# Attention's loads and broadcasts moved behind other steps of the combining sequence

## The chip, the cores and the metric

One core of a Trainium2 chip (trn2) runs the whole program. The metric is device time in microseconds (us) of one execution, the median of several runs. Lower is better.

## The reference

One decoder layer on x of shape (1, 2048, 1024) in float32. A projection gives q, k, v, two gates and the inputs of a state-space branch. The part that matters here is attention: 16 heads of 64, three dilations (1, 4, 16), each a causal band of 129 steps, and the three results weighted by a softmax over their log-sum-exps:

```python
o1, l1 = dilated_window_attention(q, k, v, slopes, DILATIONS[0])
o2, l2 = dilated_window_attention(q, k, v, slopes, DILATIONS[1])
o3, l3 = dilated_window_attention(q, k, v, slopes, DILATIONS[2])
wts = jax.nn.softmax(jnp.stack([l1, l2, l3], axis=0), axis=0)
y_att = (wts[0][..., None] * o1 + wts[1][..., None] * o2 + wts[2][..., None] * o3)
y_att = rms_norm(y_att.reshape(Bsz, S, D_ATT) * jax.nn.silu(z_att), att_norm_g[layer])
```

The state-space branch, an output projection of both branches and a layer norm follow.

## The kernel before, in words

The program has three stages. The projections with the state-space branch take the first 1163 us or so. Attention follows to about 1653 us. The output projection with its norms ends the program.

**Attention** works on the heads in 8 pairs (`pr` 0 to 7). For each pair it goes through the three dilations `d` in turn (the code's d = 0 is dilation 16, d = 1 is 4, d = 2 is 1), each in 4 quarters `qd` of 2 halves: 24 half steps for a pair. A half step is recorded in three parts at different times: `scores` (TensorE products of q and k, VectorE bias and running minimum at L955, ScalarE exponentials at L961), two half steps later `transposes` (TensorE, copied by VectorE at L978 and L987), and three half steps later `values` (TensorE products with v at L1002, and after the second half two ScalarE copies of 128x256 from PSUM into `num`, at L1026, L1029 or L1032 by dilation). TensorE runs these in the order of recording, so the scores of the next pair's first half step stand three half steps ahead of its values.

**The operands of a pair.** `load_x` brings q and k (1 MB each, two sets of buffers that alternate between pairs), `load_v` brings `v` and, for d = 1 and 2, a shifted copy `vs` (about 1 MB each, three buffers of each name). All are DMAs that GpSimd (POOL) issues (L872, L888, L890). POOL also makes permuted copies of q (`permute`, L914 and L918).

**Combining.** When a pair is through, `statistics` writes its row statistics to DRAM, `gather` reads them back (L1060, a POOL DMA), and while the next pair runs `weights` turns them into softmax weights (VectorE, one exponential on ScalarE) and writes them to DRAM (`d_wd`, L1078, a DMA issued by SyncE, SP). These are then read back as broadcasts: `wb`, 128x2048, 1 MB for each dilation, each as two DMAs of 64 partitions (L1091, SP). POOL combines in six steps k = 0 to 5 (`combine`): steps 0, 1 and 3 multiply one dilation's `num` by its `wb` (L1093), steps 2 and 4 add (L1097), step 5 multiplies by the gate (L1108), and the result goes to DRAM. For the last pair VectorE does this instead, at the beginning of the output projection.

**What sets the order.** TensorE, VectorE, ScalarE and POOL execute in the order in which the Python code records. The table `STEPS` says at which half step (d, qd, half of `values`) which combining step of the pair before is recorded and which load behind it. POOL takes its rows one after the other: a combining step that waits for its broadcast holds every load recorded behind it. SP's DMAs are in an order that a scheduler sets.

In the loop, `weights` (two parts) is recorded at (0, 2, 1) and (0, 3, 0). `STEPS` has, for pair `pr`: v and vs of its own d = 2 at (0, 0, 0) and (0, 0, 1); at (1, 0, 0) step 0 and the next pair's q; at (1, 1, 0) step 1 and the next pair's k; at (1, 2, 0) step 2 and the next pair's v for d = 0; at (1, 3, 0) step 3; at (2, 0, 0) the next pair's v for d = 1; at (2, 1, 0) step 4 and its vs; at (2, 2, 0) step 5. For pair 7 the v and vs of d = 2 stand at (1, 0, 0) and (1, 0, 1).

The output projection (`product`, L1185 to L1187) multiplies split activations (`split`, L1149 to L1153) by the output weights. Its first products need no attention result; the later ones need pair 7's combined values.

## Time and profile before

| | |
|---|---|
| median of 3 runs | 2035.58 us (2030.0 to 2038.48) |
| the profiled execution | 2040.01 us, span 2037.9 us from the first to the last instruction |
| mean granted TensorE clock | 0.985 |
| share of the span: PE, DVE, ACT, POOL | 96%, 62%, 55%, 50% |
| DMA, whole program | 447.72 MB, mean 220 GB/s |

PE is TensorE, PEld its weight loads, DVE is VectorE, ACT is ScalarE, POOL is GpSimd; SPq and the like are the sequencers that issue DMAs. In a timeline row stand the start in us from the beginning of the span, the duration, engine, line, operation, the tiles written and read, how many instructions are merged into the row, and in brackets the idle time before it with what ended it. A wait put down to "issue" is one for which the profile shows no cause. PE's busy time counts pipelined products whose ends are modelled, so 96% is not a full array.

### The profile page before, as it was taken

How to read it: one execution, taken by the hardware profiler on the slowest of the kernel's cores; microseconds unless marked ns; L12 is line 12 of the kernel's file. 1: busy time of each engine (PE TensorE's matmuls, PEld its weight loads, DVE VectorE, ACT ScalarE, POOL GpSimd, SP SyncE). 2: the span in 40 equal slices, each digit the busy share in tenths (PEclk: the TensorE clock that was granted, in tenths of full speed). 3: DMA queues.
4: the chain of work that ended last, by engine and by line, in shares of the span. 5: the costliest groups of instructions: out<-in, count | busy, mean ns of one | idle time of the engine just before them, and what ended most of it. 6: DMA issues, size and time to landing. Idle time of an engine off the chain costs nothing.

```text
span 2037.9 us, 42696 instructions
## 1 busy us (share of the span) xinstructions
PE 1961.9 (96%) x16024; PEld 1598.2 (78%) x16024; DVE 1271.4 (62%) x3193; ACT 1128.9 (55%) x3066; POOL 1010.1 (50%) x866
## 2 busy tenths in 40 slices
PE   8999999999999999999999999998989989999998
PEld 7888879888888888988888776666766668888886
DVE  7555365777766665644454387787777756665553
ACT  4455333556556774456557488887878742222220
POOL 0366513666646767155555424667766652432222
PEclk9999999999999999999999999999999989999999
DMA  6688665565787776887888756777787799332210
GB/s 265 211 281 298 221 252 215 172 197 173 244 287 276 268 256 241 306 275 249 282 269 272 250 191 198 211 215 227 222 235 223 196 309 298 122 97 103 85 67 31
DMA packets 230286, 447.72 MB, mean 220 GB/s; under 512 B 40192, under 2 KB 112384, under 8 KB 218688
## 3 DMA queue, kind: packets, MB, share of 16 engines
q1 hardware_dynamic: 138352, 190.64, 29.5%
q0 software_dynamic: 43776, 160.49, 23.3%
q10 hardware_dynamic: 47952, 93.87, 15.0%
q8 instruction: 126, 2.06, 0.4%
q14 instruction: 80, 0.66, 0.1%
HBM read 301.91 MB, written 151.39 MB: 222 GB/s over the span
## 4 chain that ended last, share of the span: by engine, by line
PE 83%; DMA 5%; DVE 5%; ACT 4%; issue 2%; SPq 1%; POOL 0%; ACTq 0%; POOLq 0%; DVEq 0%
PE pp L260 13%; PE pp L264 13%; PE pp L262 13%; PE N L1002 6%; PE S L949 4%; PE S L1185 4%; PE S L1187 4%; PE S L1186 4%; PE pp L309 4%; PE T L976 3%; ACT P L961 2%; PE T L1185 2%; PE T L1186 2%; PE T L1187 2%; PE ss L309 2%
## 5 line engine op out<-in xcount | busy, mean ns | idle before, releaser
L217 POOL TENSOR_TENSOR w<-wr,w 128x512 fp32r<-128x512 f32 x217 | 285.4, 1326 | 277.0 <-ACT w L216 182.7
L961 ACT ACTIVATE P<-P,st 128x192 f32<-128x192 f32 (+1 forms) x768 | 323.9, 424 | 71.1 <-DVE st L955 67.2
L252 ACT COPY ev<-pp 128x512 f32<-128x512 f32 x200 | 117.2, 588 | 312.5 <-PE pp L264 275.3
L955 DVE CUSTOM_DVE_ANT_0 P<-S,tb 128x192 f32<-128x192 f32 (+1 forms) x768 | 206.8, 325 | 104.5 <-PE S L949 79.9
L272 DVE TENSOR_TENSOR ev<-pp,ev 128x512 f32<-128x512 f32 x152 | 101.2, 686 | 141.4 <-PE pp L264 91.8
L1093 POOL TENSOR_TENSOR wb<-num,wb 128x2048 f32<-128x2048 f32 x21 | 95.5, 4549 | 116.2 <-ACT P L961 63.1
L216 ACT CAST w<-wr 128x512 fp32r<-128x512 f32 x224 | 134.2, 621 | 28.6 <-DVE wr L211 13.3
L961 ACT ACTIVATION_READ_ACCUMULATOR P<-P,st 128x1 f32 x768 | 145.4, 189 | 0.0
L1002 PE MATMUL N<-PT,v 128*64 128x64 f32 (+1 forms) x1536 | 127.0, 262 | 13.7 <-ACT num L1026 10.4
L978 DVE COPY PT<-T 128x512 f32<-128x512 f32 x192 | 131.8, 687 | 4.0 <-PE T L976 3.9
L976 PE MATMUL T<-ident,P 128*128 128x128 f32 x768 | 129.7, 293 | 0.2 <-DVE PT L978 0.2
L976 PEld LDWEIGHTS T<-ident,P 128*128 128x128 f32 x768 | 83.1, 144 | 48.2 <-issue 23.9
L949 PE MATMUL S<-k,ex 64*64 64x192 f32 (+1 forms) x2048 | 113.8, 331 | 6.8 <-issue 6.8
L1002 PEld LDWEIGHTS N<-PT,v 128*64 128x64 f32 x1536 | 79.4, 139 | 51.8 <-ACT num L1026 20.2
L211 DVE TENSOR_TENSOR wr<-wr 128x512 f32<-128x512 f32 x128 | 113.0, 883 | 9.3 <-DMA wr<-w 5.4
L468 DVE SCALAR_TENSOR_TENSOR ss<-U,cw,ss 128x512 f32<-128x512 f32 x144 | 106.0, 751 | 2.9 <-ACT ss L464 0.6
L1161 DVE TENSOR_REDUCE tb<-P 128x128 f32<-128x1024 f32 x30 | 60.1, 2004 | 45.4 <-ACT P L1158 23.0
L1223 POOL TENSOR_TENSOR k<-k,wb 128x1024 f32<-128x1024 f32 x8 | 25.8, 3229 | 122.7 <-DVE k L1222 122.7
L949 PEld LDWEIGHTS S<-k,ex 64*64 64x64 f32 x2048 | 68.6, 138 | 19.5 <-issue 13.3
L594 ACT ACTIVATE mt<-csb,cs 128x128 f32<-128x128 f32 x256 | 79.0, 395 | 0.9 <-PE ss L634 0.8
L603 DVE TENSOR_TENSOR mt<-mt,ss 128x1024 f32<-128x1024 f32 x32 | 39.0, 1220 | 53.3 <-ACT mt L599 52.8
L260 PE MATMUL pp<-TB11h,w 128*128 128x512 f32 x176 | 69.6, 395 | 0.0
(484 smaller groups left out, 6013.0 us busy)
## 6 DMA issues: line engine op xcount, KB each, us to landing
wr<-w ACTq DMA_DIRECT2D x164, 256.0 KB
d_wc<-w SPq DMA_DIRECT2D x48, 512.0 KB
w<-d_wc POOLq DMA_DIRECT2D x48, 512.0 KB, 5.8
wb<-d_wd SPq DMA_DIRECT2D x48, 512.0 KB
d_wo<-wot POOLq DMA_DIRECT2D x32, 512.0 KB, 4.4
csb<-d_cs ACTq DMA_DIRECT2D x32, 512.0 KB
v<-d_v POOLq DMA_DIRECT2D x16, 1024.0 KB, 7.0
vs<-d_v POOLq DMA_DIRECT2D x16, 960.0 KB, 9.0
```

What stands on the lines that cost most here:

```text
L216: nc.scalar.copy(h, r)
L217: low.tensor_tensor(l, r, h.bitcast(F32), op=OP.subtract)
L260: nc.tensor.matmul(ps, w[:, 0, k], th[:, k], start=start and k == 0, stop=False, skip_group_check=not start)
L262: nc.tensor.matmul(ps, w[:, 0, k], tl[:, k], start=False, stop=False, skip_group_check=not start)
L264: nc.tensor.matmul(ps, w[:, 1, k], th[:, k], start=False, stop=(k == 3), skip_group_check=not start)
L309: nc.tensor.matmul(o, (th, tl)[j == 1][:, k, t], w[:, int(j == 2), k], start=start and r % 2 == k == j == 0, stop=(k == 3 and j == 2), ski ...
L949: nc.tensor.matmul(o, A["q"][d][64 * h:64 * h + 64, blk, 64 * a:64 * a + 64], kv, start=True, stop=True)
L955: nc.vector.tensor_tensor_reduce(P[:, h, cs], sp[h][:, cs], t, -0.125, 3.0e38, OP.add, OP.min, accum_out=stat(A, 0, d, h, blk))
L961: nc.scalar.activation(p, p, AF.Exp, bias=stat(A, 0, d, h, blk), scale=-1.0, accum_out=stat(A, 1, d, h, blk))
L976: nc.tensor.transpose(tp[:, h, i], P[:, h, 256 * i:256 * i + 128], ident)
L978: nc.vector.tensor_copy(pt, tp)
L1002: nc.tensor.matmul(o, l, r, start=start, stop=True, skip_group_check=True)
```

## The change

It has five parts.

1. `STEPS` is rewritten. For pair `pr`, v and vs of its own d = 1 are loaded at (0, 0, 0) and (0, 0, 1), behind the gather; v of its own d = 2 behind step 0 at (1, 0, 0), vs of d = 2 behind step 1 at (1, 1, 0); the next pair's q behind step 3 at (1, 3, 0), its k behind step 4 at (2, 0, 0), its v of d = 0 behind step 5, which is now at (2, 1, 0). Pair 7 follows the same table.
2. A broadcast is one DMA of 128 partitions. Step 0's is issued by SP after the last part of the weights. Steps 0 and 1 are cut in halves of 8 rows of 16, and between the halves POOL issues the next broadcast: step 1's inside step 0, step 3's inside step 1.
3. `weights` has three parts, at (0, 2, 1), (0, 3, 0) and (0, 3, 1), so its DRAM write comes one half step later. A subtraction, two multiplications and two additions move from VectorE to POOL; two minima and the reciprocal stay. Pair 7 keeps VectorE.
4. For d = 0 the second of the two copies into `num` goes from ScalarE to VectorE.
5. In the output projection the last pair's weights are recorded behind the first product and the third split, where they stood ahead of the first product; of the output weights' loads into buffers of that time, two entries of `LOADS` move from (2, 1, 0) and (2, 1, 1) to (2, 2, 0) and (2, 2, 1).

```diff
@@ -1023,7 +1023,8 @@
                 for i in range(2):
                     nm = A["N"][i][:, 0:256]
                     if d == 0:
-                        nc.scalar.copy(f2(num[:, 4 * qd + 2 * i:4 * qd + 2 * i + 2, :]), nm)
+                        copy = nc.vector.tensor_copy if i else nc.scalar.copy
+                        copy(f2(num[:, 4 * qd + 2 * i:4 * qd + 2 * i + 2, :]), nm)
                     elif d == 1:
                         o = num.rearrange("p (b s) (n a j) -> p n b a s j", b=4, a=2, j=16)[:, qd, 2 * i:2 * i + 2]
                         nc.scalar.copy(o, nm.rearrange("p (b a s j) -> p b a s j", b=2, a=2, s=4))
@@ -1062,20 +1063,29 @@
         def weights(A, part):
 
             m_, s_ = A["cm"][:, :, 0], A["cm"][:, :, 1]
+            eng = nc.vector if A["pr"] == 7 else nc.gpsimd
             if part == 0:
                 mm = A["mm"] = cm_.tile([128, 32], F32, name="mm")
                 nc.vector.tensor_tensor(mm, m_[:, 0], m_[:, 1], op=OP.min)
                 nc.vector.tensor_tensor(mm, mm, m_[:, 2], op=OP.min)
-                nc.vector.tensor_tensor(m_, mm[:, None, :].to_broadcast([128, 3, 32]), m_, op=OP.subtract)
+                eng.tensor_tensor(m_, mm[:, None, :].to_broadcast([128, 3, 32]), m_, op=OP.subtract)
+            mm = A["mm"]
+            if part == 1:
                 nc.scalar.activation(m_, m_, AF.Exp)
-                return
-            mm = A["mm"]
-            nc.vector.tensor_tensor(s_, s_, m_, op=OP.mult)
-            nc.vector.tensor_tensor(mm, s_[:, 0], s_[:, 1], op=OP.add)
-            nc.vector.tensor_tensor(mm, mm, s_[:, 2], op=OP.add)
-            nc.vector.reciprocal(mm, mm)
-            nc.vector.tensor_tensor(m_, m_, mm[:, None, :].to_broadcast([128, 3, 32]), op=OP.mult)
-            nc.sync.dma_start(dap(d_wd[A["pr"]], 0, [[32, 128], [2 * S, 3], [1, 32]]), m_)
+                eng.tensor_tensor(s_, s_, m_, op=OP.mult)
+                eng.tensor_tensor(mm, s_[:, 0], s_[:, 1], op=OP.add)
+                eng.tensor_tensor(mm, mm, s_[:, 2], op=OP.add)
+            if part == 2:
+                nc.vector.reciprocal(mm, mm)
+                eng.tensor_tensor(m_, m_, mm[:, None, :].to_broadcast([128, 3, 32]), op=OP.mult)
+                nc.sync.dma_start(dap(d_wd[A["pr"]], 0, [[32, 128], [2 * S, 3], [1, 32]]), m_)
+
+        def broadcast(A, k):
+
+            d = k - k // 2
+            wb = A["w", k] = cm_.tile([128, NR, NJ], F32, name="wb", bufs=3)
+            (nc.sync if A["pr"] == 7 or k == 0 else nc.gpsimd).dma_start(
+                f2(wb), dap(d_wd[A["pr"]], d * 2 * S, [[S, 2], [0, 64], [1, S]]))
 
         def combine(A, k):
 
@@ -1086,11 +1096,16 @@
             pu = lambda a: a.rearrange("p (n r j) -> p r n j", r=NR, j=8)
             if k in (0, 1, 3):
                 d = k - k // 2
-                wb = A["wb"] = cm_.tile([128, NR, NJ], F32, name="wb", bufs=3)
-                for h in range(2):
-                    nc.sync.dma_start(f2(wb[64 * h:64 * h + 64]),
-                                      dap(d_wd[pr], (d * 2 + h) * S, [[0, 64], [1, S]]))
-                eng.tensor_tensor(wb, A["num"][d], wb, op=OP.mult)
+                if last:
+                    broadcast(A, k)
+                wb, num = A.pop(("w", k)), A["num"][d]
+                A["wb"] = wb
+                if last or k == 3:
+                    eng.tensor_tensor(wb, num, wb, op=OP.mult)
+                else:
+                    eng.tensor_tensor(wb[:, 0:8], num[:, 0:8], wb[:, 0:8], op=OP.mult)
+                    broadcast(A, 2 * k + 1)
+                    eng.tensor_tensor(wb[:, 8:16], num[:, 8:16], wb[:, 8:16], op=OP.mult)
                 if k == 0:
                     A["acc"] = wb
             elif k < 5:
@@ -1226,13 +1241,13 @@
 
         O = {}
         pairs = {}
-        STEPS = {(0, 0, 0): (None, "v", 0, 2), (0, 0, 1): (None, "vs", 0, 2), (1, 0, 0): (0, "q", 1),
-                 (1, 1, 0): (1, "k", 1), (1, 2, 0): (2, "v", 1, 0), (1, 3, 0): (3, None, 0), (2, 0, 0): (None, "v", 1, 1),
-                 (2, 1, 0): (4, "vs", 1, 1), (2, 2, 0): (5, None, 0)}
+        STEPS = {(0, 0, 0): (None, "v", 0, 1), (0, 0, 1): (None, "vs", 0, 1), (1, 0, 0): (0, "v", 0, 2),
+                 (1, 1, 0): (1, "vs", 0, 2), (1, 2, 0): (2, None, 0), (1, 3, 0): (3, "q", 1), (2, 0, 0): (4, "k", 1),
+                 (2, 1, 0): (5, "v", 1, 0)}
         LOADS = {(0, 0, 0): ((8, None, "k_0"),), (1, 0, 1): ((9, None, "q_0"),), (1, 1, 0): ((10, None, "ex"),),
                  (1, 2, 0): ((11, None, "vs"),), (1, 2, 1): ((12, 0, "q_1"),), (1, 3, 0): ((13, 0, "v"),),
-                 (2, 0, 0): ((14, 0, "v"), (15, 0, "vs")), (2, 1, 0): ((12, 1, None), (13, 1, None)),
-                 (2, 1, 1): ((14, 1, None), (15, 1, None))}
+                 (2, 0, 0): ((14, 0, "v"), (15, 0, "vs")), (2, 2, 0): ((12, 1, None), (13, 1, None)),
+                 (2, 2, 1): ((14, 1, None), (15, 1, None))}
         todo = [(pr, d, qd, half) for pr in range(8) for d in range(3) for qd in range(4) for half in range(2)]
         pts = {}
         TA = 2
@@ -1270,8 +1285,10 @@
                         statistics(pairs[pr], 1)
                         gather(pairs[pr])
                     at = d, qd, half
-                    if pr and at in ((0, 2, 1), (0, 3, 0)):
-                        weights(pairs[pr - 1], qd - 2)
+                    if pr and at in ((0, 2, 1), (0, 3, 0), (0, 3, 1)):
+                        weights(pairs[pr - 1], 2 * qd + half - 5)
+                    if pr and at == (0, 3, 1):
+                        broadcast(pairs[pr - 1], 0)
                     if at == (0, 0, 0) and pr < 7:
                         pairs[pr + 1] = load_pair(pr + 1)
                     if pr and at == (0, 3, 0):
@@ -1284,8 +1301,6 @@
                         split(0, 1, parts=(1,))
                     if at in STEPS:
                         k, x, nx, *dd = STEPS[at]
-                        if pr == 7 and k is None and d == 0:
-                            x = None
                         if pr and k is not None:
                             combine(pairs[pr - 1], k)
                         if x and pr + nx < 8 and (pr or nx):
@@ -1293,8 +1308,6 @@
                                 load_v(pairs[pr + nx], x, dd[0])
                             else:
                                 load_x(pairs[pr + nx], x)
-                    if pr == 7 and at in ((1, 0, 0), (1, 0, 1)):
-                        load_v(pairs[7], ("v", "vs")[half], 2)
                     if at == (2, 2, 0) and pr < 7:
                         permute(pairs[pr + 1], 1)
                     if pr < 7:
@@ -1320,8 +1333,6 @@
             squares(0, 1)
             split(1, 1)
             squares(1, 1)
-            weights(A, 0)
-            weights(A, 1)
             ops = [(n, 1) for n in range(4)] + [(n, 0) for n in range(4)]
             ops += [(n, br) for n in range(4, 16) for br in (1, 0)]
             items = [(4 * j + k, hf) for j in range(2) for k, hf in
@@ -1353,6 +1364,9 @@
                 if i in splits:
                     j = splits[i]
                     split(*ops[j])
+                    if i == 0:
+                        for n in range(3):
+                            weights(A, n)
                     squares(*ops[j])
                     for m in (j + 2,) if 4 < j < 30 else ():
                         fetch_raw(*ops[m])
```

## The prediction

> **What bounds it.** I read the page first, then TensorE's waits, then, for attention, the timelines of PE, POOL and SP beside each other.
>
> ```profile
> span 2037.9 us, 42696 instructions
> ```
>
> ```profile
> PE N L1002 <- issue: 14.2, 6, 3.2
> PE N L1002 <- ACT num L1026: 10.4, 8, 1.7
> PE S L1185 <- ACT ex L1151: 8.2, 1, 8.2
> PE S L949 <- issue: 6.8, 5, 3.4
> ```
>
> The execution took 2040.0 us, 2.1 us outside its span and 4.4 us over the median of 2035.6; I sum against 2040.0 and carry the difference over. TensorE, the engine that ends last, waits little: 21.0 us for causes the profile does not name, 10.4 us for copies at the end of d = 0, and 8.2 us once at the beginning of the output projection. So attention runs at TensorE's pace, and a load that comes in time is free. The question is whether loads still come in time. Here are the points at which TensorE needs them. The first rows are the first score products of pairs 1, 5 and 7 (they read q and k); the row at 1424.54 opens the values of d = 1 in pair 4, those with 128x128 x4 open the values of d = 2 in pairs 4 and 6, and the one with vs right behind is the first to need vs.
>
> ```profile
> 1219.17 0.62 PE L949 MATMUL S<-k,q 64*64 64x128 f32 x16
> ...
> 1424.54 0.71 PE L1002 MATMUL N<-PT,v 128*64 128x128 f32 x8 [1.57 <-ACT num L1026]
> ...
> 1445.82 0.27 PE L1002 MATMUL N<-PC,v 64*64 64x64 f32 x2 [3.22 <-issue]
> ...
> 1448.76 0.69 PE L1002 MATMUL N<-PT,v 128*64 128x128 f32 x4
> 1449.24 0.42 PE L1002 MATMUL N<-PT,vs 128*64 128x64 f32 x4
> ...
> 1460.34 0.62 PE L949 MATMUL S<-k,q 64*64 64x128 f32 x16
> ...
> 1573.27 0.44 PE L1002 MATMUL N<-PT,v 128*64 128x128 f32 x4
> ...
> 1584.04 0.62 PE L949 MATMUL S<-k,q 64*64 64x128 f32 x16
> ```
>
> Six pairs take 1584.04 - 1219.17 = 364.9 us, 60.8 each. Now POOL and SP, which feed them: the first combining steps of pairs 1, 4 and 7 are those at 1252.01, 1434.45 and 1617.49.
>
> ```profile
> 1252.01 4.55 POOL L1093 TENSOR_TENSOR wb<-num,wb 128x2048 f32<-128x2048 f32 x1 [17.89 <-DMA wb<-d_wd]
> ...
> 1416.56 1.16 POOL L890 DMA_DIRECT2D v<-d_v  x1
> 1417.70 1.21 POOL L890 DMA_DIRECT2D vs<-d_v  x1
> 1434.45 4.55 POOL L1093 TENSOR_TENSOR wb<-num,wb 128x2048 f32<-128x2048 f32 x1 [15.54 <-ACT P L961]
> 1438.94 0.60 POOL L872 DMA_DIRECT2D q<-d_q  x1
> 1440.51 4.52 POOL L1093 TENSOR_TENSOR wb<-num,wb 128x2048 f32<-128x2048 f32 x1 [0.97 <-ACT P L961]
> 1444.98 0.61 POOL L872 DMA_DIRECT2D k<-d_k  x1
> 1445.61 4.55 POOL L1097 TENSOR_TENSOR wb<-wb 128x2048 f32<-128x2048 f32 x1
> ...
> 1617.49 4.56 POOL L1093 TENSOR_TENSOR wb<-num,wb 128x2048 f32<-128x2048 f32 x1 [15.39 <-ACT P L961]
> ```
>
> ```profile
> 1241.06 0.38 SPq L1078 DMA_DIRECT2D d_wd<-cm  x1
> 1243.54 5.18 SPq L1091 DMA_DIRECT2D wb<-d_wd  x6
> ...
> 1422.07 0.38 SPq L1078 DMA_DIRECT2D d_wd<-cm  x1
> 1427.24 3.67 SPq L1091 DMA_DIRECT2D wb<-d_wd  x6
> ...
> 1673.92 2.39 SPq L1091 DMA_DIRECT2D wb<-d_wd  x4
> ```
>
> POOL idles 15.5 us for the first broadcast and starts combining at 1434.45, call it C; the exponentials named as releaser were long done. From the issue at 1427.24 to C is 7.2 us, one landing. TensorE needs vs of d = 2 at 1449.24 = C + 14.8 and the next k at 1460.34 = C + 25.9. Before, d = 2's values were issued 17 us ahead of C and k 10.5 us after it: both early.
>
> **The change, part by part.** First what stands on POOL from the first combining step on, before (d_v_84 holds d = 0 and 2, d_v_85 holds d = 1; q_62 and k_70 are the next pair's):
>
> ```order
> L890 DMA vs<-d_v_84 128x15x128
> L1093 TENSOR_TENSOR wb<-num,wb 128x2048
> L872 DMA q<-d_q_62 128x2048
> L1093 TENSOR_TENSOR wb<-num,wb 128x2048
> L872 DMA k<-d_k_70 128x2048
> L1097 TENSOR_TENSOR wb<-wb 128x2048
> L888 DMA v<-d_v_84 32x16x128 x4
> L1093 TENSOR_TENSOR wb<-num,wb 128x2048
> ```
>
> And after, at the same place, from the broadcast (L1087) that now stands between the halves of step 0 (L1106, L1108):
>
> ```order
> L1087 DMA wb<-d_wd_120 128x1x2048
> L1108 TENSOR_TENSOR wb<-num,wb 128x1024
> L890 DMA v<-d_v_84 128x16x128
> L1106 TENSOR_TENSOR wb<-num,wb 128x1024
> L1087 DMA wb<-d_wd_120 128x1x2048
> L1108 TENSOR_TENSOR wb<-num,wb 128x1024
> L890 DMA vs<-d_v_84 128x15x128
> L1112 TENSOR_TENSOR wb<-wb 128x2048
> L1104 TENSOR_TENSOR wb<-num,wb 128x2048
> L872 DMA q<-d_q_62 128x2048
> L1112 TENSOR_TENSOR wb<-wb 128x2048
> L872 DMA k<-d_k_70 128x2048
> ```
>
> The d = 2 loads went from ahead of step 0 to behind steps 0 and 1, and k from behind two steps to behind five. Durations of the loads, from the page (last number: median us to landing) and, for q and k, from their own line (least, median, most), and the loads of pair 7, whose d = 2 values already stand behind its step 0, in the chain of waits:
>
> ```profile
> v<-d_v POOLq DMA_DIRECT2D x16, 1024.0 KB, 7.0
> vs<-d_v POOLq DMA_DIRECT2D x16, 960.0 KB, 9.0
> ...
> q<-d_q POOLq DMA_DIRECT2D x8, 1024.0 KB, 9.8
> k<-d_k POOLq DMA_DIRECT2D x8, 1024.0 KB, 6.6
> ```
>
> ```profile
> DMA to landing us min/median/max: 6.0/8.5/12.0
> ```
>
> ```profile
> 1623.21 13.54 DMA vs<-d_v
> ```
>
> *The chain from C.* Half of step 0 is 2.27 (4.55 / 2), so the second broadcast is issued at C + 2.3 and, at 7.2 to landing, lets step 1 start at C + 9.5; POOL is through with its half, two issues (0.6 and 1.2) and waits 3.2. Step 1 with an issue inside is 5.15: vs of d = 2 is issued at C + 14.6 and lands 9.0 later at C + 23.6, against C + 14.8: **8.8 us late**. The issue (1.2), step 2 and step 3 (4.55 each) lead to C + 25.0, q's issue to 25.6, step 4 to 30.1; k, issued there, lands 6.6 later at C + 36.7, against C + 25.9: **10.8 us late**. The third broadcast, issued at C + 11.8, is there by C + 19 and costs nothing. The two delays overlap: from the d = 2 values to the next scores TensorE takes 1584.04 - 1573.27 = 10.8 us, or 11.6 behind the stall at 1445.82 (1448.76 to 1460.34). From vs's landing that gives C + 23.6 + 11.1 = C + 34.7, 2.0 us ahead of k. So k is last, and I take 10.8.
>
> The clock is a reason for 11.6: behind that 3.22 us stall the window (column PEclk) reads half.
>
> ```profile
> 1448.00:1450.00 2.00, 2.00 (x22) 1.55 (x24) 1.63 (x8) 1.77 (x8) 2.00 (x1) 0.50 0.78 315
> ```
>
> The Trainium skill, TensorE: Matmul & The Clock Gate (Part 1), says that about 3.4 us of idling halves the clock until some 3.4 us of work. This rule speaks against the change, whose stalls are longer; the trace agrees with 0.50 behind 3.22 us.
>
> *C itself.* On SP the six broadcast DMAs become one, before and after:
>
> ```order
> L1078 DMA d_wd_120<-cm 128x3x32
> L1091 DMA wb<-d_wd_120 64x2048 x6
> ```
>
> ```order
> L1081 DMA d_wd_120<-cm 128x3x32
> L1087 DMA wb<-d_wd_120 128x1x2048
> ```
>
> The first broadcast was first in its queue before, so 7.2 stays. The weights' write comes half a step later, 1.9 us (half of the 3.75 between the copies below). It took 5.2 us to land in pair 4 (1422.07 to 1427.24) beside v and vs, 2.5 in pair 1. Since a pair's last loads are now issued well ahead of its end, the stretch around the gather should hold less traffic, and I take pair 1's 2.5: C moves by 1.9 - 2.7 = -0.8, with +1.9 as the other end. Each of six pairs costs 10.8 - 0.8 = 10.0: **60 us**.
>
> *Pair 7.* vs landed 13.5 after its issue, at C + 19.3 (1636.75 - 1617.49). After, it is issued at C + 15.2 (an output weight's load stands ahead, 0.6) and lands 9.0 to 13.5 later, C + 26.5 in the middle: 7.2 - 0.8 = **6.4 us**.
>
> *d = 0.* Copies sit 3.75 us apart:
>
> ```profile
> 1410.97 0.62 ACT L1026 COPY num<-N 128x256 f32<-128x256 f32 x2
> 1414.72 0.61 ACT L1026 COPY num<-N 128x256 f32<-128x256 f32 x2
> ```
>
> ScalarE loses one of two (0.31) a quarter, VectorE gains one. By bounds 0.3 less or 0.3 more a quarter, 1.2 a pair; any gain ends in the wait for k, so **0**. POOL's five small weight operations lie in its 15.5 us of idling: nothing. The loads of d = 1 take the place of those at 1416.56 and 1417.70: at the medians v lands at 1423.6, ahead of its first use at 1424.54, and vs at 1426.7, before the second quarter; a microsecond late would be swallowed by the wait for vs of d = 2.
>
> *The end.* Weights behind the third split remove the 8.2 us wait for ScalarE (and slow clock behind it, some 3 us). But the products that need pair 7's result still wait for its combining.
>
> ```profile
> 1685.11 4.49 DVE L1093 TENSOR_TENSOR wb<-num,wb 128x2048 f32<-128x2048 f32 x2
> ```
>
> It can start at 1673.92 + 7.2 = 1681.1 at the earliest, 4.0 sooner: **-4 us**, between 0 and -11.4.
>
> Sum: 60 + 6.4 - 4 = +62, 2102 for the profiled execution, 2098 on the median. The good ends: 6.0 to each landing takes 3.0 off a pair (1.2, 1.2 and 0.6), pair 7 costs 1.7, the end -11.4: 42 + 1.7 - 11.4 = +32, 2068. The bad ends: 8.5 each is 4.5 more a pair, C 2.7 more, pair 7 13.9, the end 0: 6 x 17.2 + 13.9 = +117, 2153; all at once is unlikely.
>
> **Rivals.** *Faster.* POOL keeps ahead of TensorE, and bursts of six broadcast DMAs, inside which the stall at 1445.82 lies, no longer hold TensorE: 21.0 + 8.2 less, 2006. It decides once C comes 10.0 us sooner still, at 1423.7. Against it: the weights' write was only issued at 1422.07, and it and a broadcast have to land first. 0.06.
>
> *Single transfers land soon.* A transfer alone may be quicker. With x for the two broadcasts and k, a pair costs 3x - 11: 7.0 at 6.0, 1.0 at 4.0, nothing at about 3.5, where POOL's own steps bound it. That gives 2032 (the end's 4 us alone) to 2068, the middle 2050. Against it: the second broadcast, behind the first, let step 1 start 6.1 us after C, and no q or k took less than 6.0. 0.11. The Trainium skill, DMA: Bandwidth & Descriptors (Anatomy of one DMA), gives 2.0 us plus bytes over 436 GB/s, 4.4 us for such a megabyte: 2.2 a pair, 4 us less for pair 7 and 4 at the end, an estimate of 2041 by that page; no row here is that quick.
>
> *Shared queue.* vs, issued while the third broadcast runs, takes 13.5 as in pair 7: C + 14.6 + 13.5 + 11.1 = C + 39.2 becomes last, 12.5 a pair, pair 7 8.6: 75 + 8.6 - 4 = +80, 2115. 0.14.
>
> **The numbers.** The forecast has 0.69, at 2098; alone it reaches from 2068 to 2120. The range of 2052 to 2120 adds the shared queue and the slower half of soon-landing transfers. A difference of 0.5%, 10 us, is about what can be told here. Faster by more: the first rival, 0.06. Within: the lower half of the second, 0.05. Slower: 0.89.
>
> **What would show it.** In the profile after: scores of one pair to the next near 70.8 us; two waits of TensorE in each pair, for vs at d = 2's first values and for k at the next scores; POOL waiting about 3 us between steps 0 and 1; C some 35 us behind a pair's first scores, as before; no 8.2 us wait for ScalarE. I am wrong if C comes 10 us sooner, or if vs and k land before TensorE asks.

## The result, and the profile after

The changed kernel takes 2536.64 us (median of 4 runs, 2533.29 to 2541.59); the kernel before, run beside it, 2032.94 us. The ratio is 1.2476, with a 95% interval of 1.2438 to 1.2513. The forecast was 2098, the range 2052 to 2120: slower was right, the size was not, by a factor of eight in the difference. The profiled execution has a span of 2531.5 us (2037.9 before) and a mean granted clock of 0.889 (0.985 before).

First TensorE's waits after (engine, tile and line, what was waited for; then us in total, times, the longest):

```profile
PE N L1002 <- DMA v<-d_v: 259.2, 11, 38.7
PE N L1002 <- DMA vs<-d_v: 213.6, 7, 33.1
PE S L1202 <- DVE num L1168: 36.9, 1, 36.9
PE S L1200 <- ACT num L1166: 17.2, 1, 17.2
```

These four sum to 526.9 us, more than the 493.6 us by which the span grew; the waits for causes not named (21.0 before) and for the copies of d = 0 (10.4) have gone. Two long waits in each pair, where the forecast had one for vs and one for k. They are 36 and 30 us long, and they are for v of d = 2, which was to be in time, and for vs; for k TensorE waits 0.2 us in the whole program. The first scores of pairs 1 and 7, and the two waits of pair 1:

```profile
1217.51 0.62 PE L949 MATMUL S<-k,q 64*64 64x128 f32 x16
...
1297.12 0.70 PE L1002 MATMUL N<-PT,v 128*64 128x128 f32 x4 [36.47 <-DMA v<-d_v]
...
1328.09 0.48 PE L1002 MATMUL N<-PT,vs 128*64 128x64 f32 x4 [30.27 <-DMA vs<-d_v]
...
1959.08 0.62 PE L949 MATMUL S<-k,q 64*64 64x128 f32 x16
```

A pair takes (1959.08 - 1217.51) / 6 = 123.6 us, 62.8 more than the 60.8 before; the forecast had 70.8. The reason stands on SP and POOL in the same pair:

```profile
1243.46 0.58 SPq L1087 DMA_DIRECT2D wb<-d_wd  x1
```

```profile
1267.49 2.34 POOL L1106 TENSOR_TENSOR wb<-num,wb 128x1024 f32<-128x1024 f32 x1 [26.38 <-DMA wb<-d_wd]
1269.77 0.87 POOL L1087 DMA_DIRECT2D wb<-d_wd  x1
1270.67 2.35 POOL L1108 TENSOR_TENSOR wb<-num,wb 128x1024 f32<-128x1024 f32 x1
1272.95 1.22 POOL L890 DMA_DIRECT2D v<-d_v  x1
1294.52 2.33 POOL L1106 TENSOR_TENSOR wb<-num,wb 128x1024 f32<-128x1024 f32 x1 [20.34 <-DMA wb<-d_wd]
...
1325.63 4.50 POOL L1104 TENSOR_TENSOR wb<-num,wb 128x2048 f32<-128x2048 f32 x1 [19.85 <-DMA wb<-d_wd]
```

A broadcast takes 24 us to land, from 1243.46 to 1267.49, and the second one 24.8 us; the forecast had 7.2. So C comes 17 us later than a landing of 7.2 would have it, step 1 starts 27.0 us behind C in place of 9.5, and POOL waits three times in each pair. v is issued at 1272.95 behind the second broadcast, and TensorE gets it at 1297.1, just after that broadcast has landed; most of it moves soon (279 GB/s in 1276 to 1278, 49 again in 1280 to 1282), and its rest lands only with the end of the broadcast. The line of the broadcasts that POOL issues has this for all 14, and the page this for v and vs (7.0 and 9.0 before):

```profile
DMA to landing us min/median/max: 24.6/27.5/31.6
```

```profile
v<-d_v POOLq DMA_DIRECT2D x16, 1024.0 KB, 11.7
vs<-d_v POOLq DMA_DIRECT2D x16, 960.0 KB, 13.0
```

Why one megabyte takes so long is in the windows (the window, its length, busy time of PE, PEld, DVE, ACT and POOL, the granted clock, the share of the 16 DMA engines, GB/s). After, while only a broadcast runs, and later with the rest of v:

```profile
1246.00:1248.00 2.00, 2.00 (x48) 1.53 (x46) 1.67 (x9) 1.49 (x9) 0.00 (x0) 1.00 0.12 41
...
1290.00:1292.00 2.00, 0.00 (x0) 0.00 (x0) 0.00 (x0) 0.00 (x0) 0.00 (x0) 0.50 0.13 53
```

and before, in the burst of six DMAs:

```profile
1428.00:1440.00 12.00, 11.71 (x253) 8.93 (x249) 10.07 (x51) 10.40 (x46) 5.09 (x2) 1.00 1.00 218
```

The share is 0.12 to 0.13, about 2 engines of 16 (0.125), where the old form kept all of them busy. In the second row every engine of the core stands still for 2 us and the clock is at 0.50. The source of the broadcast in the diff is `[[S, 2], [0, 64], [1, S]]`: two rows, each 64 times. Before, each of the two DMAs had `[[0, 64], [1, S]]`. The Trainium skill, DMA: Bandwidth & Descriptors (Why a DMA increments its semaphore by 16 and not by 1), says that the slowest dimension of size over 1 in each of the two access patterns sets how many of the 16 engines carry a DMA, the largest count up to 16 that divides both; that gives 2 here, and the trace agrees with 0.12.

At the end of the program the last pair's three broadcasts come from SP in this form too, which makes the waits of 36.9 and 17.2 us (3.8 and 1.3 at these places in e1, whose form is the old one).

### The profile page after: what moved, and what is told of

Its sections match the earlier page's. It is cut to its first block, busy times and chain, and to the rows that moved or that the text cites. A ratio compares the mean times of both kernels' runs of the same rounds, so it can differ in the third digit from the quotient of the medians.

```text
span 2531.5 us, 42696 instructions
## 1 busy us (share of the span) xinstructions
PE 1963.3 (78%) x16024; PEld 1599.0 (63%) x16024; DVE 1271.4 (50%) x3190; ACT 1118.7 (44%) x3036; POOL 1036.4 (41%) x929
## 4 chain that ended last, share of the span: by engine, by line
PE 59%; issue 15%; DMA 13%; POOL 5%; ACT 3%; DVE 3%; SPq 0%; ACTq 0%; POOLq 0%; DVEq 0%
PE pp L260 11%; PE pp L264 11%; PE pp L262 11%; DMA wb<-d_wd 6%; DMA vs<-d_v 3%; PE S L1200 3%; PE S L1202 3%; PE pp L309 3%; PE S L1201 3%; PE N L1002 2%; ACT P L961 2%; PE S L949 2%; PE T L1200 1%; PE ss L309 1%; PE T L1201 1%
## 5 line engine op out<-in xcount | busy, mean ns | idle before, releaser
L1002 PE MATMUL N<-PT,v 128*64 128x64 f32 (+1 forms) x1536 | 127.1, 263 | 264.6 <-DMA v<-d_v 259.2
L1002 PEld LDWEIGHTS N<-PT,v 128*64 128x64 f32 x1536 | 81.1, 141 | 300.9 <-DMA v<-d_v 255.3
L1002 PE MATMUL N<-PT,vs 128*64 128x64 f32 x864 | 46.8, 230 | 213.6 <-DMA vs<-d_v 213.6
L1002 PEld LDWEIGHTS N<-PT,vs 128*64 128x64 f32 x864 | 36.9, 145 | 216.4 <-DMA vs<-d_v 216.4
L1106 POOL TENSOR_TENSOR wb<-num,wb 128x1024 f32<-128x1024 f32 x14 | 32.7, 2335 | 325.1 <-DMA wb<-d_wd 325.1
L978 DVE COPY PT<-T 128x512 f32<-128x512 f32 x192 | 131.7, 686 | 4.8 <-PE T L976 3.9
L949 PE MATMUL S<-k,ex 64*64 64x192 f32 (+1 forms) x2048 | 113.0, 331 | 0.0
L1104 POOL TENSOR_TENSOR wb<-num,wb 128x2048 f32<-128x2048 f32 x7 | 31.5, 4505 | 139.0 <-DMA wb<-d_wd 139.0
L949 PEld LDWEIGHTS S<-k,ex 64*64 64x64 f32 x2048 | 68.8, 138 | 11.7 <-issue 5.5
```

What stands on the lines that cost most here:

```text
L949: nc.tensor.matmul(o, A["q"][d][64 * h:64 * h + 64, blk, 64 * a:64 * a + 64], kv, start=True, stop=True)
L978: nc.vector.tensor_copy(pt, tp)
L1002: nc.tensor.matmul(o, l, r, start=start, stop=True, skip_group_check=True)
```

## The experiments

The diffs here are shortened: a DMA stands with its target and source alone, and `...` stands for lines left out.

Theory: the form of the broadcast (its source's first count) makes the large part of the loss, and with a sound broadcast the prediction's chain holds. Rival: serial broadcasts or the order of loads make it, by contention or POOL's order.

### The form of the broadcast

**e1: the changed kernel, each broadcast as two DMAs of 64 partitions again,** on the same queues.

```diff
-f2(wb), dap(d_wd[A["pr"]], d * 2 * S, [[S, 2], [0, 64], [1, S]])
+for h in range(2):
+    f2(wb[64 * h:64 * h + 64]), dap(d_wd[A["pr"]], (d * 2 + h) * S, [[0, 64], [1, S]])
```

> The changed kernel, but each broadcast is again two DMAs of 64 partitions, whose source has 64 as its outermost count; all else stays. Theory A (the form of the broadcast: the single DMA's source begins with a count of 2, and so only 2 of the 16 DMA engines carry the megabyte): a broadcast lands in about 7 us where it took 27.5, TensorE's waits for v and vs of d = 2 (31 and 36 us a pair) fall to about 9 us for vs, and the time is that of the prediction's steps, 2098 us (2068 to 2120). Theory B (a broadcast is slow on POOL's queue, or when it runs alone): landing stays near 27 us and the time near 2537 us.

Measured: 2116.15 us, ratio 1.0414 (1.0392 to 1.0435). The form is worth 420.5 of the 503.7 us. Its landing (of one DMA, which is half a megabyte here), the second broadcast of pair 1 from its issue to the step that needs all of it (8.3 us, against 24.8 in the changed kernel), its waits, and the first scores of pairs 1 and 7:

```profile
DMA to landing us min/median/max: 4.6/6.4/9.9
```

```profile
1252.04 1.14 POOL L1089 DMA_DIRECT2D wb<-d_wd  x2
...
1260.35 2.33 POOL L1107 TENSOR_TENSOR wb<-num,wb 128x1024 f32<-128x1024 f32 x1 [3.62 <-DMA wb<-d_wd]
```

```profile
PE N L1002 <- DMA vs<-d_v: 65.7, 7, 11.2
PE N L1002 <- DMA v<-d_v: 28.4, 12, 4.2
...
PE S L949 <- DMA k<-d_k: 6.6, 6, 2.2
```

```profile
1216.60 0.62 PE L949 MATMUL S<-k,q 64*64 64x128 f32 x16
...
1644.60 0.67 PE L949 MATMUL S<-k,q 64*64 64x128 f32 x16 [1.80 <-DMA k<-d_k]
```

A pair takes 71.3 us against the forecast's 70.8, with the wait for vs and the one for k behind it; the waits for v, which the forecast did not have, are taken up below.

**e2: the kernel before with the changed kernel's form,** `[[S, 2], [0, 64], [1, S]]`, and nothing else.

```diff
-for h in range(2):
-    f2(wb[64 * h:64 * h + 64]), dap(d_wd[pr], (d * 2 + h) * S, [[0, 64], [1, S]])
+f2(wb), dap(d_wd[pr], d * 2 * S, [[S, 2], [0, 64], [1, S]])
```

> The kernel before, with one edit: each broadcast is one DMA of 128 partitions with the source that begins with a count of 2, still issued by SP and at the old places. Theory A: three megabytes queue on two engines and land some 25, 50 and 75 us after their issue; POOL's steps and the loads behind them follow, a pair takes 100 to 115 us instead of 61 and the end some 55 us more: 2300 to 2450 us. Theory B: nothing changes, 2030 to 2040 us.

Measured: 2442.62 us, ratio 1.2018 (1.1986 to 1.2049), inside theory A's range. The form alone ruins the old order as well: the broadcasts land one behind the other (POOL's steps 0, 1 and 3 start at 1378.83, 1403.23 and 1431.34), and k stands behind step 1 on POOL:

```profile
PE S L949 <- DMA k<-d_k: 212.9, 6, 36.8
```

**e3: as e1, with the source written `[[0, 4], [0, 16], [1, S]]`:** the same bytes from the same row to the same partitions.

```diff
-    f2(wb[64 * h:64 * h + 64]), dap(d_wd[A["pr"]], (d * 2 + h) * S, [[0, 64], [1, S]])
+    f2(wb[64 * h:64 * h + 64]), dap(d_wd[A["pr"]], (d * 2 + h) * S, [[0, 4], [0, 16], [1, S]])
```

> The changed kernel, each broadcast as two DMAs of 64 partitions whose sources are written as 4 x 16 rows, so the same bytes and rows as in the two-DMA form, with an outermost count of 4. Theory A: 4 engines carry each DMA; if both take the same 4, a megabyte lands in 12 to 15 us, and with 3x - 11 us a pair the time is 2200 to 2290 us. If only the splitting into two DMAs mattered: as with 64 rows outermost, about 2098 us. If the form did not matter: about 2537 us.

Measured: 2341.4 us, ratio 1.152 (1.1489 to 1.1551), over the range that was expected. The rank was right, the price was not. A DMA of half a megabyte lands in 2.2 times e1's time, and the second broadcast of pair 1 takes 16.4 us from its issue to step 1, between 8.3 with a count of 64 and 24.8 with 2:

```profile
DMA to landing us min/median/max: 12.9/14.3/16.4
```

```profile
1268.26 1.31 POOL L1089 DMA_DIRECT2D wb<-d_wd  x2
...
1284.62 2.33 POOL L1107 TENSOR_TENSOR wb<-num,wb 128x1024 f32<-128x1024 f32 x1 [11.51 <-DMA wb<-d_wd]
```

**e10: the changed kernel with the source `[[0, 128], [1, S]]`,** one DMA.

```diff
-f2(wb), dap(d_wd[A["pr"]], d * 2 * S, [[S, 2], [0, 64], [1, S]])
+f2(wb), dap(d_wd[A["pr"]], d * 2 * S, [[0, 128], [1, S]])
```

> The kernel after with the source of each broadcast written as 128 times the first branch's row, [[0, 128], [1, S]], in place of 2 times 64: still one DMA of 128 partitions on the same queue. Both halves of the partitions so take the first branch's weights; the bytes and all work stay. Theory: the outermost count of the source decides, not that the broadcast is one DMA; it lands within 8 us, a pair takes about 70 us, TensorE waits in each pair for vs (9 us) and a little for k, and the time is near the forecast, 2095 to 2116. Rival: one DMA of 128 partitions to a queue is slow by itself, whatever its counts; 24 to 32 us to land and 2520 to 2545.

Measured: 2072.3 us, ratio 1.0187 (1.0157 to 1.0217), 23 us under the lower end of the expectation. So one DMA is no evil in itself: with a first count of 128 a whole megabyte lands in 5.7 us, sooner than the two halves of e1 together, and the waits for vs shrink from 65.7 to 44.5 us.

```profile
DMA to landing us min/median/max: 5.0/5.7/7.6
```

```profile
PE N L1002 <- DMA vs<-d_v: 44.5, 7, 8.2
```

### The order and the serial broadcasts

**e4: e1 with `STEPS`, `LOADS` and pair 7's loads of before.** Broadcasts stay single and inside halved steps.

```diff
-STEPS = {(0, 0, 0): (None, "v", 0, 1), (0, 0, 1): (None, "vs", 0, 1), (1, 0, 0): (0, "v", 0, 2),
...
+STEPS = {(0, 0, 0): (None, "v", 0, 2), (0, 0, 1): (None, "vs", 0, 2), (1, 0, 0): (0, "q", 1),
...
+if pr == 7 and at in ((1, 0, 0), (1, 0, 1)):
+    load_v(pairs[7], ("v", "vs")[half], 2)
```

> The changed kernel with two-DMA broadcasts and with the loads and the combining steps back at their places of before (the table STEPS, the table LOADS and pair 7's two loads); single broadcasts inside halved steps, the three-part weights, the copy on VectorE and the late weights of the last pair stay. Theory of order (loads behind combining steps that wait cost about 10 us a pair): 2010 to 2045 us, some 60 us less than with the new order. Rival (only the form of the broadcast cost anything): the same time as with the new order and two-DMA broadcasts, within 10 us.

Measured: 2075.98 us, ratio 1.0215 (1.0193 to 1.0238), over the range that was expected and far from the rival's: of e1's 84 us the old order takes 40 away, not all.

```profile
PE N L1002 <- DVE PT L978: 29.7, 6, 6.0
PE S L949 <- DMA k<-d_k: 11.2, 5, 3.1
```

```profile
1434.29 0.19 DVE L1069 TENSOR_TENSOR mm<-cm 128x32 f32<-128x32 f32 x1 [4.62 <-DMA cm<-d_st]
```

POOL waits 3.9 us between steps 0 and 1, so its whole row of work is later; the gather, which stands behind it, is issued later, and VectorE stands 4.6 us at the minimum that needs it. TensorE waits for the copies queued behind that minimum (L978).

**e11: the changed kernel's order and halves, but all six DMAs of 64 partitions together on SP,** none on POOL; the diff is against e1.

```diff
-queue = nc.sync if A["pr"] == 7 or k == 0 else nc.gpsimd
+queue = nc.sync
...
-                    broadcast(A, 2 * k + 1)
...
-                        broadcast(pairs[pr - 1], 0)
+                        for k in (0, 1, 3):
+                            broadcast(pairs[pr - 1], k)
```

> The kernel after, its order of steps and loads and the halved steps kept, but all six broadcast DMAs (64 partitions each) go together on SP behind the weights, as before. Theory (the prediction's chain without its 3.2 us of waiting and its issues): vs of d = 2 is issued at C + 10.3 and lands at C + 19.3, 4.5 late; k is issued at C + 25.8 and lands at C + 32.4, 6.5 late, and C itself comes 0 to 1.9 later; 6.5 to 8.4 a pair and a few us in pair 7: 2074 to 2090. Rival: most of the cost lies in waiting for the second broadcast (the kernel with the old order and serial broadcasts was already 42 us over), and the order alone costs under 15: 2036 to 2050.

Measured: 2080.48 us, ratio 1.0234 (1.0208 to 1.0259), inside the theory's range. The order costs some 46 us without serial broadcasts, these cost some 44 without the order, and both together (e1) 84. (Both runs keep the small parts of the change, which are tried alone below.)

### The small parts

**e5: the kernel before with the last pair's weights behind the third split.**

```diff
-            weights(A, 0)
-            weights(A, 1)
             ops = [(n, 1) for n in range(4)] + [(n, 0) for n in range(4)]
...
                     split(*ops[j])
+                    if i == 0:
+                        weights(A, 0)
+                        weights(A, 1)
```

> The kernel before with one part of the change alone: the weights of the last pair are made behind the third split of the tail instead of ahead of its loop. Theory (the prediction's term): the 8.2 us wait for ScalarE at the beginning of the output projection goes, the wait for the last pair's combining stays; 4 us less, between 0 and 11.4 less: 2021 to 2033, the middle 2029. Rival: the weights' write and with it the broadcasts come later, and TensorE waits for the last pair's combined parts (L1166 or L1168) instead: 2 to 10 us more, 2035 to 2043.

Measured: 2033.82 us, ratio 1.0003 (0.9993 to 1.0012). Neither: nothing gained or lost. The 8.2 us for L1185 has gone and 6.4 and 4.2 us stand behind it:

```profile
PE S L1187 <- DVE num L1153: 6.4, 3, 5.2
...
PE N L1193 <- DVE tb L1161: 4.2, 1, 4.2
```

**e6: the kernel before with every second copy of d = 0 on VectorE.**

```diff
-nc.scalar.copy(f2(num[:, 4 * qd + 2 * i:4 * qd + 2 * i + 2, :]), nm)
+copy = nc.vector.tensor_copy if i else nc.scalar.copy
+copy(f2(num[:, 4 * qd + 2 * i:4 * qd + 2 * i + 2, :]), nm)
```

> The kernel before with one part of the change alone: of the two copies of a quarter of d = 0, the second goes to VectorE. Theory: nothing, within 3 us of before, since the 10.4 us of waits for these copies would fall by at most 0.3 us a quarter and VectorE loses as much; 2030 to 2036. Rival: the waits at the end of d = 0 (10.4 us in 8 instances) vanish, 2023. Other rival: VectorE, which also makes the minima, falls behind by 0.6 a quarter: 2 a pair, 2047.

Measured: 2033.59 us, ratio 1.0001 (0.999 to 1.0011), as the theory had it.

**e7: the kernel before with the weights in three parts.**

```diff
-if pr and at in ((0, 2, 1), (0, 3, 0)):
-    weights(pairs[pr - 1], qd - 2)
+if pr and at in ((0, 2, 1), (0, 3, 0), (0, 3, 1)):
+    weights(pairs[pr - 1], 2 * qd + half - 5)
```

> The kernel before with one part of the change alone: the combining weights in three parts, five of their small operations on POOL, the write half a step (1.9 us) later; the six broadcast DMAs stay together on SP. Theory: C comes 2 to 4 us later in each pair, the next k, which was some 9 us early, stays early, and the time is the same within 4 us: 2030 to 2037; TensorE's waits for causes not named stay near 21 us. Rival: the later burst meets the stretch in which TensorE already waited 3.2 us, or POOL's small operations wait for VectorE and ScalarE by turns and C comes over 9 us later: 1 to 3 us a pair more, 2039 to 2052.

Measured: 2037.65 us, ratio 1.0023 (1.0011 to 1.0035). It lies between the two ranges, some 5 us over before by the ratio; the unnamed waits are 25.5 us (21.0 before).

### The burst, and the rate of a broadcast

Before, TensorE had 21.0 us of waits that the profile does not name, 14.2 at L1002 and 6.8 at L949. In e1, e4 and e10 they are 1.1, 4.1 and 0 us. In e11, which has waits for v, vs and k as well, they are 25.2, so other waits do not swallow them.

**e8: the kernel before with the third broadcast issued by POOL behind step 0.**

```diff
 eng.tensor_tensor(wb, A["num"][d], wb, op=OP.mult)
+if k == 0 and not last:
+    broadcast(A, 3, nc.gpsimd)
```

> The kernel before, its order of steps and loads and its form of broadcasts (two DMAs of 64 partitions each), but only the first two broadcasts go together on SP; the third is issued on POOL behind step 0, two issues of 1.1 us each, and lands some 7 us later, ahead of step 3 at about C + 17. Theory that the burst of six DMAs holds TensorE (its 21.0 us of waits for causes not named, gone where broadcasts were issued singly): most of the 21 go with a burst of four, 2012 to 2022, and those waits show under 8 us. Rival: the waits belong to something else in that stretch and stay near 21 us; then POOL's 2.2 us of issues cost nothing, 2030 to 2036. Other rival: the third broadcast, on POOL's queue ahead of k, makes the next k late as in the kernel with the old order (11 us of waits for k): 2035 to 2050.

Measured: 2037.93 us, ratio 1.002 (1.001 to 1.003); 10.3 and 5.9 us of the unnamed waits stay, and 2.4 more come at L984. A burst of four is little better than one of six.

**e12: the kernel before with three DMAs in place of six.**

```diff
-for h in range(2):
-    f2(wb[64 * h:64 * h + 64]), dap(d_wd[pr], (d * 2 + h) * S, [[0, 64], [1, S]])
+f2(wb), dap(d_wd[pr], d * 2 * S, [[0, 128], [1, S]])
```

> The kernel before with each broadcast as one DMA of 128 partitions whose source is 128 times the first branch's row, [[0, 128], [1, S]] (both halves of the partitions so take the first branch's weights; bytes and work stay): the burst on SP becomes three DMAs of the same 3 MB. Theory that the bytes of a burst hold TensorE: the waits for causes not named stay near 21 us, time as before, 2030 to 2037. Theory that the number of DMAs in the burst does: those waits halve, 2020 to 2026. Rival: C comes sooner with the quicker broadcast, POOL is ahead, and nothing of that shows: 2030 to 2037 too, with C a microsecond or two sooner.

Measured: 2011.46 us, ratio 0.9897 (0.9879 to 0.9916): the fastest run here, 21 us under before, lower than any of its theories had it. The unnamed waits:

```profile
PE S L949 <- issue: 2.4, 2, 1.4
...
PE N L1002 <- issue: 1.7, 2, 1.1
```

All DMA engines are busy, but at twice the rate of before (218 GB/s, shown above):

```profile
1422.00:1428.00 6.00, 6.00 (x152) 4.71 (x148) 5.34 (x24) 5.41 (x24) 3.83 (x1) 1.00 1.00 414
```

**e14: e4 with the source `[[0, 128], [1, S]]`.**

```diff
-for h in range(2):
-    f2(wb[64 * h:64 * h + 64]), dap(d_wd[A["pr"]], (d * 2 + h) * S, [[0, 64], [1, S]])
+f2(wb), dap(d_wd[A["pr"]], d * 2 * S, [[0, 128], [1, S]])
```

> The kernel with the old order of steps and loads and broadcasts singly, each as one DMA with the source [[0, 128], [1, S]] (both halves of the partitions take the first branch's weights). Theory: what the old order lost with two DMAs to a broadcast (42 us) came from the wait between steps 0 and 1 and the issues on POOL, some 3 us a pair shorter here (7.7 us from step 0 to step 1 in place of 10.2); the gather is issued in time, VectorE's waits of 4.6 to 5.5 us for it fall under 2, and about half to all of the loss goes: 2032 to 2055. Rival: with TensorE's unnamed waits also gone it is faster than before: 2012 to 2028. Other rival: POOL's order and not its waiting sets the gather, the time stays at 2066 to 2078.

Measured: 2027.42 us, ratio 0.9968 (0.9952 to 0.9984), inside the range of the rival that it is faster than before, by 0.3%. VectorE's late copies still cost 23.9 us, the unnamed waits are 0.6.

Open was why one DMA of 128 partitions is twice as quick as two of 64: the half of the partitions, the number of DMAs, or the one row that it reads. Three runs of one change each to the kernel before:

**e16: two DMAs, to the even and to the odd partitions.**

```diff
-nc.sync.dma_start(f2(wb[64 * h:64 * h + 64]),
+nc.sync.dma_start(f2(wb[h:128:2]),
```

> The kernel before with the two DMAs of a broadcast writing the even and the odd partitions in place of the lower and the upper 64 (the weights of the two branches so come to other partitions; bytes, rows read, number of DMAs and all work stay). Theory that the half of the partitions sets the rate: the burst runs near 400 GB/s in place of 218, is over in 8 us in place of 15, the waits for causes not named go under 6 us, 2009 to 2018. Rival, the number of DMAs or the reading of two rows: as before, 218 GB/s, waits near 21 us, 2030 to 2037. The Trainium skill, SBUF - State Buffer (Door 1: The DMA port swizzle), has partitions 0 to 63 on 8 of 16 ports and 64 to 127 on the other 8, which would be the theory.

Measured: 2019.0 us, ratio 0.993 (0.991 to 0.995), a microsecond outside the expected range; the unnamed waits are 1.4 us. Six DMAs that read both rows are quick when each spreads over all 128 partitions:

```profile
1427.00:1431.00 4.00, 4.00 (x105) 3.13 (x102) 3.67 (x18) 3.93 (x17) 3.32 (x1) 1.00 0.98 397
```

The Trainium skill, SBUF - State Buffer (Door 1: The DMA port swizzle), has partitions 0 to 63 on 8 of the 16 ports and measures 196 GB/s for them against 328 for all 128; that is a ratio of 0.60, and 218 against 397 and 414 is one of 0.53 to 0.55 here.

**e17: lower halves on SP, upper halves on POOL's queue.**

```diff
+for h, queue in enumerate((nc.sync, second)):  # second: nc.gpsimd, for pair 7 nc.sync
+    queue.dma_start(f2(wb[64 * h:64 * h + 64]), dap(d_wd[A["pr"]], (d * 2 + h) * S, [[0, 64], [1, S]]))
```

> The kernel before with the lower halves of its three broadcasts on SP and the upper halves on POOL's queue, all issued ahead of step 0 (the last pair as before). All of the reference is computed. Theory that the halves then run side by side: the burst runs near 400 GB/s, the waits not named go, 2009 to 2020, faster than before. Rival: the halves still come one behind the other on the 16 engines, the burst runs near 218 GB/s, 2030 to 2040; POOL's 1.6 us of issues cost nothing. The Trainium skill, SBUF - State Buffer (Can I just issue two DMAs to hit both halves?), has two such DMAs only 6% quicker than one, which would be the rival.

Measured: 2039.79 us, ratio 1.003 (1.0016 to 1.0044); 20.0 us of unnamed waits. The rival holds: with two queues the burst still runs at 205 to 262 GB/s.

```profile
1436.00:1438.00 2.00, 2.00 (x48) 1.53 (x46) 1.67 (x9) 1.92 (x10) 0.00 (x0) 1.00 1.08 246
```

**e15: each row copied 8 times in DRAM, the broadcast one DMA with the source `[[S, 16], [0, 8], [1, S]]`,** which computes all of the reference.

```diff
+nc.sync.dma_start(dap(d_we[A["pr"]][d], 0, [[S, 8], [8 * S, 2], [1, S]]),
+                  dap(d_wd[A["pr"]], 2 * d * S, [[0, 8], [S, 2], [1, S]]))
...
+nc.sync.dma_start(f2(wb), dap(d_we[pr][d], 0, [[S, 16], [0, 8], [1, S]]))
```

> The kernel before; in pairs 0 to 6 each of the two rows of a broadcast is first copied 8 times in DRAM (one DMA to each d, 128 KB, on SP behind the weights' write), and each broadcast is then one DMA of 128 partitions with the source [[S, 16], [0, 8], [1, S]]; the last pair keeps its two DMAs. All of the reference is computed. Theory: the source's 16 rows keep all engines at work and the 128 partitions the full rate, so a broadcast lands in 5 to 6 us as with 128 times one row; the copies put C 2 to 5 us later, which the next k (some 9 us early) bears; the 21 us of waits not named go: 2011 to 2022, faster than before. Rival: the copies and a second round through DRAM take over 9 us, k comes late: 2035 to 2060. Other rival: reading one row was what made the broadcasts quick, the bursts stay long, the waits stay: 2032 to 2040.

Measured: 2052.86 us, ratio 1.0103 (1.0082 to 1.0125): the theory fell. The time is in the first rival's range: C comes 10.8 us behind the first copy's issue (1439.53 to 1450.35); but TensorE waits 19.6 us for VectorE's copies, as in e4, and hardly for k. The second rival's sign is there too: the unnamed waits are 19.7 us, and the burst is slow though each DMA has 128 partitions.

```profile
1449.00:1451.00 2.00, 2.00 (x52) 1.48 (x50) 1.74 (x10) 1.92 (x10) 0.65 (x1) 1.00 0.97 209
```

**e18: the kernel before with one DMA, one row, but `[[0, 16], [0, 8], [1, S]]`.**

```diff
-for h in range(2):
-    f2(wb[64 * h:64 * h + 64]), dap(d_wd[pr], (d * 2 + h) * S, [[0, 64], [1, S]])
+f2(wb), dap(d_wd[pr], d * 2 * S, [[0, 16], [0, 8], [1, S]])
```

> The kernel before with each broadcast as one DMA of 128 partitions, all from the first branch's row as in the run with three DMAs, but with the source written [[0, 16], [0, 8], [1, S]] in place of [[0, 128], [1, S]] (both halves of the partitions so take the first branch's weights; bytes and work stay). Theory: how the source is split decides how the rows are dealt to the DMA engines; the burst runs at 209 to 250 GB/s as with 16 rows times 8, the waits for causes not named come back to some 20 us, 2028 to 2037. Rival: reading one row is what makes it quick; 400 GB/s, waits under 6 us, 2009 to 2016.

Measured: 2030.52 us, ratio 0.9988 (0.9975 to 1.0); unnamed waits 14.8 and 5.8 us, as before:

```profile
1430.00:1438.00 8.00, 8.00 (x174) 6.13 (x166) 7.06 (x34) 7.00 (x31) 1.86 (x1) 1.00 1.01 223
```

So it is not the reading of one row: the same row to the same partitions runs at 414 GB/s as 128 and at 223 as 16 times 8. How the source is split sets the rate even where all engines are at work. By the ports of that section of the Trainium skill (SBUF - State Buffer, Door 1: The DMA port swizzle) alone, a DMA to all 128 partitions would have had the full rate here; the measurement decides.

## Why the prediction was wrong

**The step that failed** is the sentence "The first broadcast was first in its queue before, so 7.2 stays", and with it every broadcast behind it. The 7.2 us belonged to two DMAs of 64 partitions with a first count of 64. The change had made it one DMA with a first count of 2, which is in the diff and, as 128x1x2048, in the order that the prediction quotes; the price was taken over by tile and bytes, without a look at the access pattern. It measured 24.0 for the first broadcast of pair 1, and 27.5 in the median of POOL's 14. In e1, with the old form, the first broadcast in pair 4 took 7.1:

```profile
1457.61 1.12 SPq L1089 DMA_DIRECT2D wb<-d_wd  x2
```

```profile
1464.70 2.37 POOL L1107 TENSOR_TENSOR wb<-num,wb 128x1024 f32<-128x1024 f32 x1 [8.94 <-DMA wb<-d_wd]
...
1475.21 2.34 POOL L1107 TENSOR_TENSOR wb<-num,wb 128x1024 f32<-128x1024 f32 x1 [3.51 <-DMA wb<-d_wd]
```

None of the rivals had a broadcast slower than 8.5 us, and with all bad ends at once the sum reached 2153.

**The steps of the chain,** judged by e1, where the broadcasts are sound. *Step 1 at C + 9.5, a wait of 3.2:* 10.5 and 3.5 (1475.21 - 1464.70). *vs 8.8 late:* 8.6 to 9.6 in pairs 1 to 6, but behind a wait of 1.9 to 3.0 for v, which the prediction had in time. In pair 4:

```profile
1478.30 0.44 PE L1002 MATMUL N<-PT,v 128*64 128x128 f32 x4 [2.99 <-DMA v<-d_v]
...
1487.31 0.48 PE L1002 MATMUL N<-PT,vs 128*64 128x64 f32 x4 [8.58 <-DMA vs<-d_v]
...
1501.63 0.67 PE L949 MATMUL S<-k,q 64*64 64x128 f32 x16 [2.17 <-DMA k<-d_k]
```

The loads themselves end where the prediction put them: with C at 1464.70, vs lands at C + 22.6 (23.6 forecast) and k at C + 36.8 (36.7). That is errors cancelling: they were issued at C + 16.2 and C + 31.5, some 1.5 later than in the chain, and landed in 6.4 and 5.3 in place of 9.0 and 6.6. What was mis-sized is the moment of need. The C + 14.8 came from pair 4 before, whose rows hold the stall of 3.22 at 1445.82; in e1 that stall is gone, and TensorE stands at the first values of d = 2 at C + 10.6 (1478.30 - 2.99), so it waits for v as well.

*k last, by 2.0:* 1.1 in the mean of six waits, 2.2 at most, behind the one for vs. *C moves by -0.8, +1.9 at the other end:* about right. In the mean of pairs 1 to 6 it stands 34.5 us behind the first scores in e1 and before; in pair 4 it stands 36.2 behind them (1428.51) and stood 34.8 behind them before:

```profile
1399.61 0.62 PE L949 MATMUL S<-k,q 64*64 64x128 f32 x16
```

```profile
1428.51 0.67 PE L949 MATMUL S<-k,q 64*64 64x128 f32 x16 [1.41 <-DMA k<-d_k]
...
1438.90 0.69 PE L1002 MATMUL N<-PT,v 128*64 128x128 f32 x8 [2.21 <-DMA v<-d_v]
```

The weights' write of pair 4 was issued 27.3 behind the scores in e1 (1455.79) and 22.5 before (1422.07), 4.8 later in place of 1.9; its landing was 3.4 shorter (1.8 for 5.2), as argued. Of those 4.8, 2.2 is the wait for d = 0's v at 1438.90, whose load is now behind step 5: a term that the prediction did not have.

*10.0 a pair:* 10.5, near by errors that cancel. In these six pairs of e1 TensorE waits 54.5 us for vs, 22.1 for v and 6.6 for k, 13.9 a pair; but 18.1 us of unnamed waits and 8.6 for the copies of d = 0, 4.5 a pair, have all but gone, and of the unnamed ones only the first rival had spoken. So e1 inside the forecast's range is in part luck. *Pair 7, 6.4:* its waits are 4.2 for v and 11.2 for vs, and C stands 37.5 behind its first scores where it stood 33.5.

**The small terms.** *The copies of d = 0, 0:* right (e6). *The weights' small operations, nothing:* some 5 us in e7 (0.2%), together with the later write. *The end, -4:* 0 (e5). That the products which need pair 7 would still wait was seen; that they would take back all 8.2 was the bad end of the range.

**The rivals.** The first one's premise was right, its place not: the burst is what holds TensorE, worth 21 us in e12 and 13 in e16, but not by POOL coming ahead. Single transfers that land soon are real too: q and k land in 5.2 us in the median of e1's 16, where none took less than 6.0 before; the broadcast comes to 5.7 only in another form of source (e10). (That rival's estimate of 2041 counts 4 us of gain in pair 7, where TensorE had waited 0.1 us for vs; without it its terms give some 2045.) The shared queue did not show in e1, where vs of d = 2 took 6.4 to 6.7 us in pairs 1 to 6 although the third broadcast ran. In the changed kernel it did, far dearer: in pair 1 vs, issued at 1299.98, came at 1328.09, behind the third broadcast at 1325.63.

**What stays open.** Why slow bursts hold TensorE was not put to a run. The unnamed waits are 18 to 26 us in all nine kernels that issue broadcasts in bursts of halves or of 16 times 8 (before, e5, e6, e7, e8, e11, e15, e17, e18) and under 5 in those with quick bursts (e12, e16) or single broadcasts (e1, e4, e10, e14). The traces point to the fetching of TensorE's instructions. Two DMA queues are of the kind "instruction", and one of them, q8, moves packets of 16 KB. Before, in pair 4, only q1, the queue of the broadcasts, started packets from 1434 to 1443, though POOL had issued q at 1438.94; then a packet on q8 starts at 1443.00, and TensorE, which stood since 1442.6, goes on at 1445.82. Lines of the two stretches, 1434 to 1443 and 1443 to 1444.5 (packets, MB, share of the engines):

```profile
q1 hardware_dynamic: 319, 1.86, 99.8%
```

```profile
...
q8 instruction: 1, 0.02, 5.6%
...
```

All 105 unnamed waits of 0.5 us or more in attention, over all kernels here, end 2.2 to 3.0 us after the start of a packet on q8, while 10 to 13% of TensorE's other instructions start that far behind one. That they are waits for instructions, and that the burst makes the packets late, fits these rows, but no run here tests it by itself. No version that computes all of the reference beat the kernel before: the quick forms send one branch's weights to both halves, or the two branches' to other partitions. One DMA with a first count of 64 and both halves in its second dimension was not tried.

## What to carry to other kernels

A landing time belongs to a DMA's access pattern, not to its tile and bytes: before a row's duration is used for a changed DMA, compare the counts of both patterns, the outermost first. Where a transfer is priced, look at two things in the windows while it runs alone, the share of the DMA engines and the GB/s: here a share of 0.12 came with a first count of 2, and a share of 1 at half the rate with halves of the partitions or a source split as 16 times 8. Where a moment of need is read from the profile before, ask whether a stall that the change removes stands ahead of it. And a load that is moved behind a step inherits everything that this step can wait for.

## What the hardware showed that I had not expected

- A DMA of 1 MB to 128 partitions landed in 27.5 us with a first count of 2 and in 5.7 with 128; as two DMAs of half a megabyte, each landed in 14.3 with a count of 4 and in 6.4 with 64. From the issue of a whole megabyte to the step that needs it, pair 1's second broadcast took 24.8, 16.4 and 8.3 us with 2, 4 and 64.
- At a full share of the DMA engines, broadcasts ran at 218 GB/s to lower and upper halves, at 223 with a source of 16 times 8, and at 397 to 414 with even and odd partitions or a source of 128.
- During bursts at the lower rate TensorE lost some 3 us a pair (18.1 in six pairs before) to waits without a named cause, and next to nothing during bursts at the higher one. All of those of 0.5 us or more ended 2.2 to 3.0 us after the start of a 16 KB packet on the DMA queue of the kind "instruction".
